# The last layer's residual: turned by DMA in 16-bit halves and added by DMA, instead of by TensorE transposes

## The chip, the cores and the metric

The kernel runs on one core of a Trainium2 chip. The metric is the device time of one execution in microseconds (us); the median of several executions is compared. One execution of each kernel was also recorded by the hardware profiler, and all rows shown here come from such a record. TensorE is PE in the rows (PEld its weight loads), VectorE is DVE, ScalarE is ACT, GpSimd is POOL, and SyncE, which only issues DMAs in this kernel, is SP.

## The reference

Two layers on a sequence of 1024 tokens with 1024 channels, everything in float32. Layer 0 is a gated delta-rule attention, layer 1 a chunked softmax attention; each is followed by the same convolutional FFN. What matters here is the end of layer 1:

```python
def conv_ffn(xn, w_up, conv_w, conv_b, w_down):
    h = causal_dwconv(xn @ w_up, conv_w) + conv_b
    gate, val = h[..., :FFN_DIM], h[..., FFN_DIM:]
    return (jax.nn.silu(gate) * val) @ w_down
...
        h = h + conv_ffn(rmsnorm(h, f_norm[layer]), f_w_up[layer], f_conv[layer], f_conv_b[layer], f_w_down[layer])
    return rmsnorm(h, final_norm)
```

The output has tokens in rows. The `h` that is added in the last line but one is the residual this text is about. Inside the kernel it lies with channels on the 128 partitions and tokens along the free axis, so that it has to be transposed before the final norm.

## The kernel before

Both FFNs are written by one function, `ffn(layer, ...)`. Every float32 product is made of three matmuls on a high and a low part (`uh`/`ul` from the raw up-weights `r`, `dh`/`dl` from the raw down-weights `a`, `eh`/`el` from the gated hidden rows `val`): high times high, low times high, high times low. ACT casts the high part, POOL or DVE subtracts to get the low part. The up-product and the down-product are done by a scheme of seven half-size products (n = 1 to 7) in place of eight.

The order of work is written by hand. `step(key, f)` appends one piece of PE work to the list `seq`; nearly every step is 12 matmuls with 512 columns. `at(i, f, rank)` hangs work for the other engines and DMA issues onto step i; at each step the jobs are emitted by rank, then the PE work. Each engine runs its own instructions in the order of emission and waits where an input is not there. SP's queue is such an order too: a DMA behind one that waits for a buffer is issued after it.

- `load` (L1492) and `load_a` (L1755) issue the weight loads on SP, some steps ahead.
- `product` and `second` are the up- and down-products on PE. The result of `second` is copied to `stage` and sent by POOL (`send`, L1817, and `send_e`, L1824) with an accumulating DMA into the DRAM tiles `d_c`, which gather the down-product of groups 0 to 8 (two hidden tiles of 128 channels each, 18 of the 22; the last four are done apart).
- `end` is the last step of the up-products. After it come the steps `("f", t)`: for each of the eight token tiles t the last four hidden tiles times their down-weights (`fw`, cut into `fh`/`fl` by `cut_last`), accumulated in PSUM tiles `pf`. These are laid out with tokens on the partitions already.
- Before the change, each pair (t, half c) of `pf` starts with the residual: `load_r` loads a 128x4x128 piece of `d_r` (the DRAM copy of the residual that layer 1's attention wrote, `d_r1`), and `tile_of` transposes it on PE into the PSUM tile with `is_transpose=True` (L1974), so that the products add onto it.
- `load_t` (L1944) loads the gathered sums of token tile t from `d_c` into the SBUF tile `fh[t]` (called `ht` in the rows). `closing(t)` adds the PSUM tile onto it on DVE and then runs the steps of the final norm `norm_out`: the squares on ACT, the reciprocal and the scaling on DVE, the output DMAs on SP.

At the start of the kernel the input x is turned in a similar way to what the change now does for the residual: DMA transposes of x seen as 16-bit halves into `xm` (L1280), a store to DRAM (L1282), a load of the halves (L1291), and copies of each half to every second 16-bit place (L1299). There POOL and DVE make the copies.

Of the kernel before, what the change touches and what calls it, by code (L numbers as in the profile page):

```python
# [9 lines left out]
F32 = mybir.dt.float32  # L10
# [6 lines left out]
P = 128  # L17
# [11 lines left out]
def trunk_kernel(  # L29
# [92 lines left out]
    def hs(s):  # L122
        return slice(s * HALF, (s + 1) * HALF)
# [375 lines left out]
    ctx_h = ExitStack()  # L499

    d_r0 = {(c, s, u): dram.tile([P, SEQ], F32, name=f"d_r0{c}{s}{u}") for c in range(2) for s in range(2) for u in range(2)}
    d_r1 = {(c, s): dram.tile([P, 2 * SEQ], F32, name=f"d_r1{c}{s}") for c in range(2) for s in range(2)}
    quarter = lambda d, m, s: d[m // 4, s, m % 4 // 2][:, hs(m % 2)] if (0, 0, 0) in d else d[m // 4, s][:, hs(m % 4)]
    d_y = [[dram.tile([P, HALF], F32, name=f"d_y{k}_{s}") for s in range(2)] for k in range(KT)]
    d_z = [[dram.tile([P, HALF], F32, name=f"d_z{k}_{s}") for s in range(2)] for k in range(KT)]
# [901 lines left out]
    def ffn(layer, h, hp, xs, tail, d_r, last):  # L1407
# [475 lines left out]
        if layer == 0:  # L1883

            def part(s, m, ks):
                def f():
                    if ks[0] == 0:
                        if s == 0 and m > 3:
                            if m % 2 == 0:
                                fps["d"] = pacc.tile([P, SEQ], F32, name="pf", tag="d", bufs=2)  # L1890
                            fps[s, m] = fps["d"][:, hs(m % 2)]
                        else:
                            fps[s, m] = pacc.tile([P, HALF], F32, name="pf", tag="u", bufs=4)
                    for k in ks:
                        triple(fps[s, m], fw[m], [t_[:, hs(s)] for t_ in hid[k0 + k]], kc[k], k == 0, k == 3)
                        if (s, m, k) in ((1,5,3),(1,6,2)):
                            next(norms[0])
                return f

            def closing(s, m):  # L1900
                def f():
                    tt(nc.vector, fh[m][:, hs(s)], fps[s, m], fh[m][:, hs(s)], add)
                    nc.sync.dma_start(out=d_h[m][:, hs(s)], in_=fh[m][:, hs(s)])
                    if m == 0:
                        norms.append(norm_steps(fh, s, None, last))
                    next(norms[s])
                    if s == 1 and m > 5:
                        for _ in range((2, 8)[m - 6]):
                            next(norms[0], None)
                return f  # L1910

            for m in range(KT):
                step(("f", 0, m, 0), part(0, m, range(3)))
            for m in range(KT):
                step(("f", 0, m), part(0, m, range(3, 4)))
            for m in range(KT):
                step(("f", 1, m), part(1, m, range(4)))
            for s in range(2):
                for m in range(KT):
                    at(pos["f", s, m | 1 if s == 0 and m > 3 else m] + 1, closing(s, m), 0)  # L1920

            def fin_h():
                for m in range(KT):
                    fh[m] = fin.tile([P, SEQ], F32, name=f"h{m}", tag=f"h{m}")
                for s in range(2):
                    for m in range(KT):
                        nc.sync.dma_start(out=fh[m][:, hs(s)], in_=quarter(d_c, m, s))
                rooms = [x for _ in range(3) for x in ("uh", "ul")]

                def tmp():  # L1930
                    rooms.append(rooms.pop(0))
                    return wf.tile([P, HALF], F32, name="nt", tag=rooms[-1], bufs=3)

                env["tmp"] = tmp
                env["acc"] = lambda s: wf.tile([P, HALF], F32, name="nacc", tag="dh", bufs=2)
                env["aux"] = lambda name: pacc.tile([P, SEQ], F32, name=name, tag="d", bufs=2)

            at(end, fin_h, 3)
        else:

            def load_t(t):
                fh[t] = fin.tile([P, SEQ], F32, name=f"ht{t}", tag=f"ht{t}")
                for c in range(2):
                    nc.sync.dma_start(out=fh[t][:, hs(c)], in_=d_c[c, t // 4, t % 4 // 2][:, hs(t % 2)])  # L1944

            res = {}

            def load_r(t):

                for c in range(2):  # L1950
                    if t < 4:
                        tag = ("eh", "el", "dh", "dl")[t % 2 * 2 + c]
                        r_ = (wd if tag[0] == "e" else wf).tile([P, 4, P], F32, name="res", tag=tag, bufs=2)
                    else:
                        r_ = actp.tile([P, 4, P], F32, name="res", tag=f"x{'hl'[c]}{t}_1")
                    nc.sync.dma_start(out=r_, in_=d_r[c, t // 4].rearrange("p (f t) -> p f t", f=4)[:, :, kc[t % 4]])
                    res[t, c] = r_

            def tile_of(t, ks):
                def f():  # L1960
                    if ks[0] == 0:
                        if t in (0, 1, 4, 5):
                            ps = pacc.tile([P, SEQ], F32, name="pf", tag="d", bufs=2)
                            fps[t] = [ps[:, hs(c)] for c in range(2)]
                        else:
                            fps[t] = [pacc.tile([P, HALF], F32, name="pf", tag="u", bufs=4) for _ in range(2)]
                            if t == KT - 1:
                                fps[t].append(pacc.tile([P, SEQ], F32, name="pf", tag="d", bufs=2))
                    for c in range(2):
                        parts = [(fps[t][c], 0, HALF)] if (t, c) != (KT - 1, 1) else [(fps[t][1 + q], 256 * q, 256) for q in range(2)]  # L1970
                        for ps, o, n in parts:
                            if ks[0] == 0:
                                for f in range(n // P):
                                    nc.tensor.matmul(ps[:, f * P : (f + 1) * P], res[t, c][:, o // P + f], ident, is_transpose=True, start=f == 0, stop=False, skip_group_check=True)  # L1974
                            for k in ks:
                                hh, hl = [x_[:, t * P : (t + 1) * P] for x_ in hid[k0 + k]]
                                hi, lo = [x_[:, o : o + n] for x_ in fw[2 * k + c]]
                                mm(ps[:, 0:n], hh, hi, start=False, stop=False, skip_group_check=True)
                                mm(ps[:, 0:n], hh, lo, start=False, stop=False, skip_group_check=True)
                                mm(ps[:, 0:n], hl, hi, start=False, stop=k == 3, skip_group_check=True)  # L1980
                return f

            its = {}

            def closing(t):
                def f():
                    its[t] = last(t, fh[t], fin)
                    if t == KT - 1:
                        tt(nc.vector, fh[t][:, hs(0)], fps[t][0], fh[t][:, hs(0)], add)
                        next(its[t - 1], None)  # L1990
                        next(its[t])
                        for q in range(2):
                            part = fh[t][:, HALF + 256 * q : HALF + 256 * (q + 1)]
                            tt(nc.vector, part, fps[t][1 + q][:, 0:256], part, add)
                            next(its[t], None)
                        return
                    for c in range(2):
                        tt(nc.vector, fh[t][:, hs(c)], fps[t][c], fh[t][:, hs(c)], add)
                    next(its[t])
                    if t > 0:  # L2000
                        next(its[t - 1], None)
                return f

            for t in range(4):
                step(("f", t, 0), tile_of(t, range(3)))
            for t in range(4):
                step(("f", t), tile_of(t, range(3, 4)))
            for t in range(4, KT):
                step(("f", t), tile_of(t, range(4)))
            at(end, lambda: last(None, None, fin), 3)  # L2010
            for t in range(KT):
                at(pc[t] if t < 4 else end + 1, lambda t=t: load_r(t), 3.5)
                at(end, lambda t=t: load_t(t), 4)
                at(pos["f", t] + 1, closing(t), 0)

        with tc.manual_schedule():
            for i in range(len(seq) + 8):
# [32 lines left out]
    with ExitStack() as ph:  # L2050
# [402 lines left out]
        def rest(s):  # L2453
# [20 lines left out]
            for m in range(KT):  # L2474
# [8 lines left out]
                nc.vector.tensor_tensor(h[m][:, hs(s)], ps, h[m][:, hs(s)], op=ALU.add)  # L2483

                def then(s=s, m=m):
                    nc.scalar.dma_start(out=quarter(d_r1, m, s), in_=h[m][:, hs(s)])
                    if m == 0:
                        its[s] = norm_steps(h, s, g_f[:, 1], normed, keep=True, gap=s == 0)
                    next(its[s])
# [153 lines left out]
```

## Time and profile before

| what | value |
|---|---|
| median of 3 executions | 2516.37 us (2515.14 to 2516.85) |
| the profiled execution: its time, its span in the trace | 2516.6 us, 2514.9 us |
| TensorE clock granted | 0.998 |
| busy share of the span: PE, DVE, POOL, ACT | 99%, 73%, 60%, 56% |
| packets on SP's DMA queue | 228.77 MB, 31.0% of the 16 DMA engines' span |
| packets of POOL's DMAs (nearly all accumulating) | 94.38 MB, 21.0% |

The span is the time from the first to the last instruction of the trace; the 1.7 us between it and the execution's own time lie before and after. In a timeline row stand the start in us, the duration, the engine, the line, the operation, out<-in, the shape, and in brackets how long the engine was idle before it and what ended that. In a row on DMAs "to landing" is the time from issue to the arrival of the data. Layer 1's FFN runs from about 1880 us to the end, and the steps ("f", t) from 2456.8 us.

### The profile page before, as it was taken

The page shows a single profiled execution, that of the slowest core. Times are in us where ns is not written, and L with a number is a line of the kernel's source. Part 1 is how long each engine was busy: PE and PEld are TensorE (multiplying, and loading weights), DVE is VectorE, ACT ScalarE, POOL GpSimd, SP SyncE. Part 2 cuts the span into 40 slices and gives each one's busy share as a digit, 9 for nine tenths or more (in the row PEclk, how much of TensorE's full clock was granted, in tenths as well). Part 3 has the DMA queues.
Part 4 walks back from the last instruction along what each step waited for, and adds up shares of the span by engine and source line. Part 5 has one row for each costly group of instructions (what it writes and reads, how often), then busy time and mean ns, then how long its engine had stood idle before and what let it go on. Part 6 is the DMA issues. An engine that isn't in the chain of part 4 may idle for free.

```text
span 2514.9 us, 39318 instructions
## 1 busy us (share of the span) xinstructions
PE 2483.2 (99%) x13905; PEld 2070.7 (82%) x13905; DVE 1835.3 (73%) x2984; ACT 1408.7 (56%) x2708; POOL 1496.6 (60%) x1523
## 2 busy tenths in 40 slices
PE   8999999999999999999999999999999999999999
PEld 6888888888878888888888888888877888888877
DVE  5765774456798888888866556667489788888884
ACT  6444555464465556565555556566456555655553
POOL 3655553357457777777635544445444777777770
PEclk9999999999999999999999999999999999999999
DMA  8743444554347777767832111122432667777795
GB/s 227 190 116 105 133 128 146 162 184 148 100 106 145 151 153 152 152 143 158 190 133 63 54 57 49 49 68 79 139 101 92 157 142 153 151 153 150 153 197 187
DMA packets 334101, 334.31 MB, mean 133 GB/s; under 512 B 50000, under 2 KB 256336, under 8 KB 333904
## 3 DMA queue, kind: packets, MB, share of 16 engines
q1 hardware_dynamic: 303232, 228.77, 31.0%
q0 software_dynamic: 25920, 94.38, 21.0%
q10 hardware_dynamic: 4752, 8.65, 1.0%
q8 instruction: 109, 1.79, 0.3%
q14 instruction: 88, 0.72, 0.1%
HBM read 180.68 MB, written 146.87 MB: 130 GB/s over the span
## 4 chain that ended last, share of the span: by engine, by line
PE 90%; POOL 3%; issue 2%; DVE 2%; ACT 1%; DMA 1%; SPq 0%; POOLq 0%; DVEq 0%; ACTq 0%
PE pu L1448 9%; PE pu L1446 9%; PE pu L1447 9%; PE acc L118 8%; PE acc L119 8%; PE acc L120 8%; PE pd L1447 4%; PE pd L1448 4%; PE pd L1446 4%; PE acco L118 2%; PE acco L120 2%; PE acco L119 2%; PE ptp L2272 2%; POOL ul L1412 1%; PE poT L2318 1%
## 5 line engine op out<-in xcount | busy, mean ns | idle before, releaser
L1412 POOL TENSOR_TENSOR ul<-r,uh 128x512 fp32r<-128x512 f32 x267 | 429.9, 1629 | 260.2 <-ACT uh L1434 255.3
L118 PE MATMUL acc<-xh,whi 128*128 128x512 f32 x896 | 374.9, 419 | 0.6 <-ACT xh L1094 0.6
L119 PE MATMUL acc<-xl,whi 128*128 128x512 f32 x896 | 352.3, 393 | 0.5 <-POOL xl L381 0.4
L120 PE MATMUL acc<-xh,wlo 128*128 128x512 f32 x896 | 351.9, 393 | 0.0
L103 POOL TENSOR_TENSOR wlo<-wraw,whi 128x256 fp32r<-128x256 f32 (+1 forms) x326 | 238.4, 761 | 140.1 <-ACT whi L101 132.8
L1434 ACT CAST uh<-r 128x512 fp32r<-128x512 f32 x289 | 177.3, 622 | 183.8 <-DVE r L1412 153.3
L1448 PE MATMUL pu<-xh,ul 128*128 128x512 f32 x524 | 204.6, 390 | 0.9 <-POOL ul L1412 0.9
L1446 PE MATMUL pu<-xh,uh 128*128 128x512 f32 x524 | 204.4, 390 | 0.7 <-ACT keep L1575 0.7
L1802 ACT COPY stage<-pd 128x1024 f32<-128x1024 f32 x180 | 175.3, 1013 | 53.0 <-PE pd L1448 51.6
L1447 PE MATMUL pu<-xl,uh 128*128 128x512 f32 x524 | 203.9, 389 | 0.0
L120 PEld LDWEIGHTS acc<-xh,wlo 128*128 128x128 f32 x896 | 168.5, 188 | 37.7
L119 PEld LDWEIGHTS acc<-xl,whi 128*128 128x128 f32 x896 | 169.6, 189 | 25.3 <-POOL xl L381 2.4
L118 PEld LDWEIGHTS acc<-xh,whi 128*128 128x128 f32 x896 | 169.3, 189 | 24.2 <-ACT xh L1094 1.0
L2227 POOL TENSOR_SCALAR sS<-sS,st 128x640 f32<-128x640 f32 (+4 forms) x128 | 86.0, 677 | 173.2 <-DVE st L2225 161.3
L1412 POOL TENSOR_TENSOR dl<-a,dh 128x512 fp32r<-128x512 f32 x90 | 151.9, 1687 | 53.6 <-ACT dh L1434 42.3
L1541 DVE SCALAR_TENSOR_TENSOR gate<-gpre,colt,gate 128x1023 f32<-128x1023 f32 (+2 forms) x92 | 173.3, 1884 | 3.2 <-ACT gate L1538 2.4
L1541 DVE SCALAR_TENSOR_TENSOR val<-vpre,colt,val 128x1023 f32<-128x1023 f32 x88 | 147.7, 1678 | 28.9 <-ACT val L1538 28.8
L2217 DVE CUSTOM_DVE_ANT_0 sS<-sc,bt 128x640 f32<-128x640 f32 (+4 forms) x128 | 84.2, 658 | 111.3 <-PE sc L2213 86.6
L1412 DVE TENSOR_TENSOR r<-r,r 128x512 f32<-128x512 f32 x160 | 130.3, 814 | 31.2 <-POOL ul L1412 30.1
L1412 DVE TENSOR_TENSOR el<-val,eh 128x512 fp32r<-128x512 f32 x90 | 86.0, 955 | 43.3 <-ACT eh L1434 43.3
L1448 PEld LDWEIGHTS pu<-xh,ul 128*128 128x128 f32 x524 | 98.3, 188 | 23.3 <-POOL ul L1412 1.8
L1446 PEld LDWEIGHTS pu<-xh,uh 128*128 128x128 f32 x524 | 98.4, 188 | 21.2 <-ACT keep L1575 1.1
(422 smaller groups left out, 7161.7 us busy)
## 6 DMA issues: line engine op xcount, KB each, us to landing
r<-in_f_w_up_dram SPq DMA_DIRECT2D x176, 256.0 KB, 4.3
d_r<-stage POOLq DMA_DIRECT2D x78, 512.0 KB, 7.9
d_c<-stage POOLq DMA_DIRECT2D x70, 512.0 KB, 8.0
a<-in_f_w_down_dram SPq DMA_DIRECT2D x72, 256.0 KB, 2.7
wraw<-in_a_w_in_dram SPq DMA_DIRECT2D x32, 512.0 KB, 4.6
d_e<-stage POOLq DMA_DIRECT2D x32, 512.0 KB, 9.2
wraw<-in_a_w_out_dram SPq DMA_DIRECT2D x16, 512.0 KB, 3.9
d_r<-h ACTq DMA_DIRECT2D x32, 256.0 KB, 2.5
```

Of the source, the lines that this page charges most:

```text
L103: nc.gpsimd.tensor_tensor(lo[:, c], raw[:, c], hi[:, c].bitcast(F32), op=ALU.subtract)
L118: mm(ps, hi[:, kw, wcol : wcol + P], rh[k][s], start=st, stop=False)
L119: mm(ps, hi[:, kw, wcol : wcol + P], rl[k][s], start=False, stop=False)
L120: mm(ps, lo[:, kw, wcol : wcol + P], rh[k][s], start=False, stop=sp)
L1412: tt = lambda eng, o, a, b, op: eng.tensor_tensor(o, a, b, op=op)
L1434: copy(hi, src)
L1446: mm(ps, w[0][:, cw], x[0], start=first, stop=False, skip_group_check=True)
L1447: mm(ps, w[0][:, cw], x[1], start=False, stop=False, skip_group_check=True)
L1448: mm(ps, w[1][:, cw], x[0], start=False, stop=last, skip_group_check=True)
L1541: nc.vector.scalar_tensor_tensor(t_[:, a:c1], p_[:, a - step : c1 - step], w[:, 2 - step : 3 - step], t_[:, a:c1], op0=ALU.mult, op1=ALU.add)
L1802: nc.scalar.copy(t_, ps)
L2227: nc.gpsimd.tensor_scalar(S, S, st[:, 3:4], 1.0, op0=ALU.mult, op1=ALU.mult)
```

## The change

The residual is stored row by row in one DRAM tile, turned during layer 1's FFN, and loaded into the final tiles as float32 with tokens on the partitions. The gathered sums `d_c` are then added onto it in SBUF by accumulating DMAs of POOL. The transposes on PE and their loads are gone, and the first matmul of each `pf` tile starts the accumulation.

```diff
-    d_r1 = {(c, s): dram.tile([P, 2 * SEQ], F32, name=f"d_r1{c}{s}") for c in range(2) for s in range(2)}
+    d_r1 = dram.tile([SEQ, SEQ], F32, name="d_r1")
...
             def load_t(t):
                 fh[t] = fin.tile([P, SEQ], F32, name=f"ht{t}", tag=f"ht{t}")
+                nc.sync.dma_start(out=fh[t], in_=d_rj[t])
+
+            def add_t(t):
                 for c in range(2):
-                    nc.sync.dma_start(out=fh[t][:, hs(c)], in_=d_c[c, t // 4, t % 4 // 2][:, hs(t % 2)])
-
-            res = {}
-
-            def load_r(t):
-
-                for c in range(2):
-                    if t < 4:
-                        tag = ("eh", "el", "dh", "dl")[t % 2 * 2 + c]
-                        r_ = (wd if tag[0] == "e" else wf).tile([P, 4, P], F32, name="res", tag=tag, bufs=2)
-                    else:
-                        r_ = actp.tile([P, 4, P], F32, name="res", tag=f"x{'hl'[c]}{t}_1")
-                    nc.sync.dma_start(out=r_, in_=d_r[c, t // 4].rearrange("p (f t) -> p f t", f=4)[:, :, kc[t % 4]])
-                    res[t, c] = r_
+                    nc.gpsimd.dma_start(out=fh[t][:, hs(c)], in_=d_c[c, t // 4, t % 4 // 2][:, hs(t % 2)], accum_op=add)
+
+            U16 = mybir.dt.uint16
+            d_rt = [dram.tile([2 * SEQ, HALF], U16, name=f"d_rt{c}") for c in range(2)]
+            d_rj = [dram.tile([P, SEQ], F32, name=f"d_rj{t}") for t in range(KT)]
+            rows_u = d_r.bitcast(U16)
+            turned, parts_r = {}, {}
+
+            def turn_r(b, c):
+                turned[b, c] = tp.tile([P, HALF], U16, name="rm", tag="rm", bufs=2)
+                nc.sync.dma_start(out=turned[b, c], in_=rows_u[hs(c), b * P : (b + 1) * P], transpose=True)
+
+            def put_r(b, c):
+                nc.sync.dma_start(out=d_rt[c][b * P : (b + 1) * P], in_=turned[b, c])
+
+            def load_r(t, c, q):
+                r_ = parts_r[t, c, q] = tp.tile([P, 2, 256], U16, name="rm", tag="rm", bufs=2)
+                nc.sync.dma_start(out=r_, in_=d_rt[c].rearrange("(t h) c -> t h c", h=2)[t * P : (t + 1) * P, :, q * 256 : (q + 1) * 256])
+
+            def join_r(t, c, q):
+                r_ = parts_r[t, c, q]
+                f_ = parts_r[t, c, q] = tp.tile([P, 256], F32, name="rj", tag="rm", bufs=2)
+                hm = f_.bitcast(U16).rearrange("p (t h) -> p t h", h=2)
+                for i in range(2):
+                    nc.scalar.copy(hm[:, :, i], r_[:, i])
+
+            def send_r(t, c, q):
+                nc.sync.dma_start(out=d_rj[t][:, c * HALF + q * 256 : c * HALF + (q + 1) * 256], in_=parts_r[t, c, q])
...
-                            if ks[0] == 0:
-                                for f in range(n // P):
-                                    nc.tensor.matmul(ps[:, f * P : (f + 1) * P], res[t, c][:, o // P + f], ident, is_transpose=True, start=f == 0, stop=False, skip_group_check=True)
...
-                                mm(ps[:, 0:n], hh, hi, start=False, stop=False, skip_group_check=True)
+                                mm(ps[:, 0:n], hh, hi, start=k == 0, stop=False, skip_group_check=True)
...
-                at(pc[t] if t < 4 else end + 1, lambda t=t: load_r(t), 3.5)
                 at(end, lambda t=t: load_t(t), 4)
+                at(end + 2, lambda t=t: add_t(t), 4.5)
                 at(pos["f", t] + 1, closing(t), 0)
+            i = pos["p", 3, 7]
+            for o in range(16):
+                for c in range(2):
+                    at(i, lambda o=o, c=c: turn_r(o, c), 3.2)
+                    at(i + 2, lambda o=o, c=c: put_r(o, c), 3.2)
+                    i += 2
+            i += 2
+            for t in range(KT):
+                for c in range(2):
+                    for q in range(2):
+                        at(i, lambda t=t, c=c, q=q: load_r(t, c, q), 3.2)
+                        at(i + 2, lambda t=t, c=c, q=q: join_r(t, c, q), 2.6)
+                        at(i + 3, lambda t=t, c=c, q=q: send_r(t, c, q), 3.1)
+                        i += 3
```

The first place that moves is ScalarE in the middle of the layer, where the 32 joins stand between the casts, seven of them in a period of 57 us that repeats. These are its instructions at one place of that period, before:

```order
L1538 ACTIVATE gate<-gpre,colt 128x1024
L1575 COPY keep<-pu_22380 128x512
L1434 CAST uh<-r_22166 128x512
L1434 CAST dh<-a_21932 128x512
L1434 CAST eh<-val 128x512
L1434 CAST uh<-r_22214 128x512
L1434 CAST uh<-r_22351 128x512
```

And the same place after (`rm` are the loaded halves, `rj` the joined float32 piece):

```order
L1971 COPY rj<-rm 128x256 x2
L1575 COPY keep<-pu_22542 128x512
L1434 CAST uh<-r_22310 128x512
L1434 CAST dh<-a_22055 128x512
L1434 CAST eh<-val 128x512
L1434 CAST uh<-r_22361 128x512
L1971 COPY rj<-rm 128x256 x2
L1434 CAST uh<-r_22510 128x512
```

Two copies stand ahead of the drain `keep` and its cast, and two more ahead of the cast of the next weights, six instructions later.

The second place is SP's queue at the same time, before:

```order
L1492 DMA r_22351<-in_f_w_up_dram 128x4x128
L1755 DMA a_22353<-in_f_w_down_dram 128x512
L1755 DMA a_22355<-in_f_w_down_dram 128x512
L1492 DMA r_22425<-in_f_w_up_dram 128x4x128
L1755 DMA a_22427<-in_f_w_down_dram 128x512
L1492 DMA r_22449<-in_f_w_up_dram 128x4x128
```

And after, where the first `r` is the same load as the first one above:

```order
L1492 DMA r_22510<-in_f_w_up_dram 128x4x128
L1755 DMA a_22512<-in_f_w_down_dram 128x512
L1755 DMA a_22514<-in_f_w_down_dram 128x512
L1974 DMA d_rj_19543<-rj 128x256
L1964 DMA rm<-d_rt_19540 128x2x256
L1492 DMA r_22590<-in_f_w_up_dram 128x4x128
L1755 DMA a_22592<-in_f_w_down_dram 128x512
L1492 DMA r_22617<-in_f_w_up_dram 128x4x128
L1974 DMA d_rj_19543<-rj 128x256
L1964 DMA rm<-d_rt_19540 128x2x256
```

The store of a joined piece, which waits for ScalarE, and the next load of halves now stand between the weight loads.

The third place is POOL behind its last subtractions, before:

```order
L1412 TENSOR_TENSOR ul<-r_24540,uh 128x512
L1412 TENSOR_TENSOR fl_24719<-fr,fh_24718 128x512
L1412 TENSOR_TENSOR fl_24794<-fr,fh_24793 128x512
L2558 TENSOR_TENSOR ht_24777<-ht_24777,g_fin 128x512
L2639 UNCONDITIONAL_BRANCH
```

And after:

```order
L1412 TENSOR_TENSOR fl_24998<-fr,fh_24997 128x512
L1412 TENSOR_TENSOR fl_25065<-fr,fh_25064 128x512
L1947 DMA ht_25035<-d_c_19477 128x512
L1947 DMA ht_25035<-d_c_19481 128x512
L1947 DMA ht_25037<-d_c_19477 128x512
L1947 DMA ht_25037<-d_c_19481 128x512
```

Sixteen accumulating DMAs follow the last subtraction on POOL, of which the first four are shown; before, POOL had nothing to do there until the end.

More of the change, by code (lines that the diff above doesn't have):

```diff
@@ L2485, in then @@
                 def then(s=s, m=m):
-                    nc.scalar.dma_start(out=quarter(d_r1, m, s), in_=h[m][:, hs(s)])
+                    nc.scalar.dma_start(out=d_r1[m * P : (m + 1) * P, hs(s)], in_=h[m][:, hs(s)])
                     if m == 0:
```

## The prediction

> **What bounds the kernel now.** I read the page first, then the busy time by stretch, then PE's and DVE's timelines at the end.
>
> ```profile
> span 2514.9 us, 39318 instructions
> PE 2483.2 (99%) x13905; PEld 2070.7 (82%) x13905; DVE 1835.3 (73%) x2984; ACT 1408.7 (56%) x2708; POOL 1496.6 (60%) x1523
> PE 90%; POOL 3%; issue 2%; DVE 2%; ACT 1%; DMA 1%; SPq 0%; POOLq 0%; DVEq 0%; ACTq 0%
> ```
>
> PE is busy for 99% of the span and makes 90% of the chain that ended last. The kernel gets shorter only by work taken off PE, or longer by waits that PE does not have now. The stretches of layer 1's FFN (columns: PE, PEld, DVE, ACT, POOL busy, granted clock, DMA share, GB/s) say where there is room:
>
> ```profile
> 2060.00:2120.00 60.00, 59.88 (x264) 49.20 (x264) 51.15 (x48) 35.70 (x51) 47.04 (x35) 1.00 0.69 145
> 2360.00:2400.00 40.00, 39.95 (x176) 32.57 (x175) 33.63 (x29) 21.38 (x29) 32.16 (x26) 1.00 0.91 185
> 2440.00:2456.00 16.00, 15.23 (x67) 12.64 (x68) 12.38 (x9) 7.43 (x12) 9.55 (x6) 1.00 1.10 297
> 2456.00:2480.00 24.00, 24.00 (x123) 19.73 (x122) 8.52 (x13) 4.78 (x9) 1.73 (x2) 1.00 0.82 259
> ```
>
> In the middle PE loses 0.1 us in 60, at 264 matmuls, so a step of 12 is 2.73 us. ACT is busy for 60% of it, and the DMA engines for 69%. With the DMA share at 0.91 PE still loses only 0.05 us in 40. From 2456 us on PE never stops.
>
> **The transposes leave PE.** The timeline of PE at the end:
>
> ```profile
> 2456.77 0.60 PE L1974 MATMUL pf<-ident,res 128*128 128x128 f32 x4
> 2459.29 0.60 PE L1974 MATMUL pf<-ident,res 128*128 128x128 f32 x4
> 2476.93 0.39 PE L1978 MATMUL pf<-fh,hidh 128*128 128x512 f32 x1
> 2482.54 0.60 PE L1974 MATMUL pf<-ident,res 128*128 128x128 f32 x4
> 2485.76 0.60 PE L1974 MATMUL pf<-ident,res 128*128 128x128 f32 x4
> ```
>
> Four transposes and 9 matmuls take 2459.29 - 2456.77 = 2.52 us. Between 2476.93 and 2482.54 stand the 24 matmuls of the last k of tiles 0 to 3, which have no transposes: 0.2338 us each. Nine of them make 2.10, so four transposes cost 0.42 us. Later, with 12 matmuls, it is 3.22 - 2.81 = 0.41. There are 16 such groups, 6.7 us in all. Not all of it reaches the end, as DVE shows:
>
> ```profile
> 2478.53 2.69 DVE L1412 TENSOR_TENSOR ht<-pf,ht 128x512 f32<-128x512 f32 x4 [11.47 <-PE pf L1980]
> 2495.64 1.29 DVE L1412 TENSOR_TENSOR ht<-pf,ht 128x512 f32<-128x512 f32 x2 [3.22 <-PE pf L1980]
> 2505.31 0.69 DVE L1412 TENSOR_TENSOR ht<-pf,ht 128x512 f32<-128x512 f32 x1 [1.01 <-PE pf L1980]
> 2507.44 0.42 DVE L1412 TENSOR_TENSOR ht<-pf,ht 128x256 f32<-128x256 f32 x1
> ```
>
> The closings wait for PE up to the first half of tile 7 at 2505.31; the next at 2507.44 comes with no idle time, behind DVE's scaling of tile 6. So 15 of the 16 groups count: 15 x 0.42 = 6.3 us. Bounds: 5.9 (14 groups) and 6.7.
>
> **The loads of `res` go.** Half of these 16 loads (4.2 MB) were issued before 2456 us, where the DMA engines have no room (share 1.10). PE's one large wait there:
>
> ```profile
> PE pul L1448 <- POOL ul L1412: 1.2, 1, 1.2
> POOL d_c L1824 <- DMA d_c<-stage: 5.5, 1, 5.5
> ```
>
> POOL stood 5.5 us for the landing of an accumulating DMA, and its next `ul` came 1.2 us late. Two `res` loads (0.5 MB) run beside that DMA and go. The gain lies between 0 and 1.2; I take 0.3, since 0.5 MB is a small part of what is in flight.
>
> **Turning and storing, 32 of each, on SP's queue.** A pair stands every second step, 5.4 us. Nearest rows are the transposes of x, of twice the size, each with its time to landing, and the first loads of halves:
>
> ```profile
> L1280 SPq DMA_TRANSPOSE xm<-in_x_dram x16: 1159/1292/6231, 11.6 to 73.2; - x16
> ...
> DMA to landing us min/median/max: 3.1/3.7/7.8
> L1291 SPq DMA_DIRECT2D xm<-d_xt x16: 529/540/1017, 80.8 to 636.8; - x16
> ...
> DMA to landing us min/median/max: 3.0/4.1/5.0
> ```
>
> A store waits for its transpose, so a pair holds SP for 3.7 us and the store's issue of about 0.4, which fits into 5.4. Behind it wait weight loads, and behind those ACT's casts. A typical one with little room:
>
> ```profile
> 2172.68 0.37 SPq L1492 DMA_DIRECT2D r<-in_f_w_up_dram  x1
> 2184.98 1.39 ACT L1434 CAST uh<-r 128x512 fp32r<-128x512 f32 x2
> ```
>
> The waits of SP's queue in the 12.7 us up to it (total, times, longest):
>
> ```profile
> SPq L1492 <- POOL ul L1412: 6.5, 1, 6.5
> SPq L1492 <- DVE r L1412: 1.2, 1, 1.2
> ```
>
> The load issued at 2172.68 feeds the second of these casts, at 2185.7: 13 us, of which some 4 are flight. Nine us are left for delay in the queue, two whole pairs. Three pairs stand ahead of such a load at the worst, of which the first store finds its data landed: 9 us by these rows, against the 6.5 + 1.2 = 7.7 that SP waits there for buffers now. I take 0; bounds 0 and 4 us (two such places, 2 us each).
>
> The traffic of the whole chain is four passes of 4.2 MB, 16.8 MB, over some 160 steps or 437 us. At the rate of SP's queue (228.77 MB in 31.0% of the span, 293 GB/s of engine time; rows below) that is 57 us, a share of 0.13: from 0.69 to about 0.82, under the 0.91 at which PE did not wait.
>
> **Joining, 32 times two copies on ACT.** ACT has a copy of this width in the norm's squares; DVE's joins of x are the same operation over 512 elements:
>
> ```profile
> 2507.94 0.42 ACT L2556 ACTIVATE jk<-ht 128x256 f32<-128x256 f32 x1 [0.85 <-DVE ht L1412]
> L1299 DVE COPY xs<-xm x16: 454/750/1285, 545.4 to 645.9; 128x512 uint16<-128x512 uint16 x16
> ```
>
> Two copies make 0.84 us, within DVE's 0.45 to 1.29 for as many elements; I take 0.84, ACT's own row. That is 27 us of ACT over 262 us, in which it is idle for 40%. It matters where the cast behind it has little time to reach PE, as at the `keep` in the place shown above:
>
> ```profile
> 2181.86 0.56 ACT L1575 COPY keep<-pu 128x512 f32<-128x512 f32 x1
> 2183.13 0.62 ACT L1434 CAST uh<-r 128x512 fp32r<-128x512 f32 x1 [0.70 <-DVE r L1412]
> 2183.83 1.75 POOL L1412 TENSOR_TENSOR ul<-r,uh 128x512 fp32r<-128x512 f32 x1 [1.46 <-ACT uh L1434]
> 2186.18 0.39 PE L1448 MATMUL pu<-xt2h,ul 128*128 128x512 f32 x1
> ```
>
> A delay of `keep` is first taken up by the 0.70 us for which ACT waits for DVE, then by the 0.60 between the end of `ul` (2185.58) and its use. That is 1.30 against 0.84: hidden, with 0.46 to spare. This is the tightest of the seven places that repeat. What can break it is the load of halves: issued when the store before it is, about 3 us before the second join of this place by the row of 2184.98, it lands after 4.1. ACT would stand 1 to 2 us there; but POOL is busy with the `ul` and `dl` before, and the cast has time. I put 0.5 us for all joins; bounds 0 and 7 (five `keep` places, 1.4 each).
>
> The page "DMA: Bandwidth & Descriptors" of the Trainium skill, section "Anatomy of one DMA", fits a DMA's time as 2.0 us and its bytes at 436 GB/s. As an estimate from that page, a load of 128 KB would land after 2.3 us and no join would wait, and the sum would end 0.5 us lower. The measured 4.1 (for 256 KB, where that fit gives 2.6) says that loads here take longer, and decides.
>
> **The gathered sums are added by POOL's DMAs.** The rows for it:
>
> ```profile
> q1 hardware_dynamic: 303232, 228.77, 31.0%
> q0 software_dynamic: 25920, 94.38, 21.0%
> q1 hardware_dynamic: 3072, 4.42, 105.3%
> L1817 POOL DMA_DIRECT2D d_c<-stage x64: 848/900/1493, 1981.4 to 2426.7; - x64
> 2452.12 11.57 SPq L1944 DMA_DIRECT2D ht<-d_c  x16
> 2461.14 1.29 POOL L1412 TENSOR_TENSOR fl<-fr,fh 128x512 fp32r<-128x512 f32 x1 [4.70 <-ACT fh L1874]
> ```
>
> The third row is the 12 us from 2452, nearly all `ht` loads: 4.42 MB, 368 GB/s. The accumulating DMAs run at 94.38 MB in 528 us, 179 GB/s. After the change SP starts the residual's 4.2 MB at 2452.1; with 0.9 MB of other loads they are in by 2466. POOL is free at 2462.4 and issues 16 DMAs at 0.9 us, until 2477. The adds need 4.2 MB / 179 = 23.5 us of the DMA engines; with about 1.8 done before 2466 and 2 us to land, tile t is complete at about 2469 + 3t: tile 0 at 2469, tile 3 at 2478, tile 7 at 2490. Needed are tile 0 at 2478.5 - 8 x 0.42 = 2475.2, tiles 1 to 3 at 1.4 us each behind it (2479.4), tile 7 at 2501.1. So the adds are hidden, with 11 us to spare at the end and hardly any at tile 3; a tile that is late there costs nothing, since DVE is idle between later closings. Bounds: nothing, if adding into SBUF runs as the sends into DRAM did; with half that rate tile 7 lands at 2513.2, 12.1 us too late. I take 0, the rate of the only accumulating rows.
>
> **The sum.** -6.3 (transposes) - 0.3 (`res`) + 0 (turning) + 0.5 (joins) + 0 (adds) = -6.1 us, from 2514.9 to 2508.8 of span. The profiled execution took 2516.6, 1.7 more than its span and 0.2 more than the median, so the median becomes 2516.37 - 6.1 = 2510.3.
>
> **Rivals.** First, the middle pays it back: ACT stands at the joins, or weight loads come late behind SP's stores. For it speaks that ACT runs in order and everything behind a join waits; against it the idle 40% of ACT. At its bound of 7 us, or half of that with the 4 us of turning, the time is 2512 to 2517: no measurable change.
>
> Second, slower: the adds end last. The place is closing of tile 7, the price 23.5 us times a factor for SBUF as the target. It costs nothing up to a factor of 1.48 (tile 7 at 2501.1), eats the whole gain at 1.75, and at 2 gives 2516.37 - 6.1 + 12.1 = 2522.4. For it: such a DMA is not in this trace, and its rows are 2 KB where the sends had 4 KB. Against it: the sends' rate already holds reads of the target, from DRAM.
>
> Third, a little more: all of POOL's 1.2 us wait goes and all 16 groups count, 2516.37 - 6.7 - 1.2 = 2508.5.
>
> **How the numbers follow.** The forecast's own range is 2508.9 to 2511.3, chance 0.60; the third case (2508 to 2508.9) 0.06; the first rival (2511.3 to 2517) 0.23; the adds last (2513 to 2525) 0.11. What can be told from no change is 0.2%, 5.0 us: faster is under 2511.3, slower over 2521.4. Faster 0.66; same 0.23 and about 0.02 of the adds, 0.25; slower 0.09. The range 2508.4 to 2517 leaves out most of the adds' case and the end of the third: it holds 0.87.
>
> **What would show it.** No L1974 of PE, the pitch of the `pf` groups at 2.10 and 2.81 us, and a last closing 6 us earlier: the first term. PE at 59.9 of 60 in the stretches from 1940 to 2360, with no row of PE waiting for ACT, POOL or DVE over 2 us in sum: the middle is hidden. No idle time of DVE's `ht` from tile 4 on that ends by a DMA: the adds are in time; such a row of several us at tile 7 means the second rival. The prediction is wrong if PE's busy share falls in the middle, or if the closings wait for `ht`.

## The result, and the profile after

The changed kernel is slower: 2525.58 us median of 22 executions (2516.32 to 2533.77), against 2516.76 of 22 before (2513.74 to 2521.48). The ratio is 1.0032, with a 95% interval of 1.0021 to 1.0042. The forecast was 2510.3, at most 2517. The profiled execution of the changed kernel took 2519.74 us, 5.8 less than the median, so its trace shows the kinds of loss, and less of it than most executions have.

The page of the changed kernel, the same three rows as shown of before:

```profile
span 2518.0 us, 39436 instructions
PE 2479.6 (98%) x13841; PEld 2063.7 (82%) x13841; DVE 1833.4 (73%) x2984; ACT 1429.1 (57%) x2772; POOL 1506.6 (60%) x1539
PE 80%; DMA 7%; issue 4%; POOL 4%; DVE 4%; ACT 2%; SPq 0%; ACTq 0%; DVEq 0%; POOLq 0%
```

PE's share of the chain that ended last fell from 90% to 80%, and DMA rose from 1% to 7%. The stretches say where (same columns as in the prediction; the last row is the kernel before, at the time of the second):

```profile
2060.00:2120.00 60.00, 57.52 (x248) 45.57 (x247) 45.01 (x45) 34.74 (x52) 42.29 (x33) 1.00 0.86 182
2180.00:2240.00 60.00, 57.08 (x248) 45.80 (x247) 46.39 (x45) 38.36 (x62) 43.21 (x33) 1.00 0.76 168
2360.00:2400.00 40.00, 40.00 (x177) 32.87 (x177) 33.89 (x32) 24.25 (x37) 30.38 (x26) 1.00 0.94 202
2456.00:2480.00 24.00, 23.84 (x105) 19.44 (x104) 16.47 (x18) 10.84 (x16) 12.64 (x13) 1.00 0.82 260
...
2180.00:2240.00 60.00, 59.99 (x264) 49.28 (x264) 49.80 (x48) 36.14 (x51) 46.23 (x34) 1.00 0.72 148
```

Before, PE did at least 264 matmuls in each 60 us of the middle; now it does 248 in two of them. Both kernels run the same 13,841 matmuls once the transposes are left out, so each can be matched with its own in the other trace. Its start after less its start before, worked out so:

```
matmul    before     after    after - before
 12065   2095.17   2096.36      +1.2
 12091   2101.35   2104.36      +3.0    while it is turned
 12139   2112.38   2116.38      +4.0    behind the first join
 12319   2153.18   2157.92      +4.7
 12595   2216.27   2225.69      +9.4
 13099   2331.33   2342.39     +11.1    joining, to 2372 us
 13567   2440.76   2450.44      +9.7    one PE wait of 1.2 us is gone
 13638   2457.44   2467.11      +9.7    the last products begin
 13701   2475.09   2481.39      +6.3
 13830   2507.11   2509.86      +2.8    the last tile
```

From the first of the last products on PE gains 6.9 us, where 6.3 was forecast; the span is 3.1 us longer than before, so 6.6 of the gain reach its end. The middle loses 11: it stands at +0.3 when turning begins at 1910 us, so some 3 us are lost while the residual is turned and 8 from the first join on. The waits of ScalarE and of PE that have to do with it, from 2060 to 2360 us (total, times, longest):

```profile
ACT rj L1971 <- DMA rm<-d_rt: 20.9, 11, 5.2
ACT rj L1971 <- DMA r<-in_f_w_up_dram: 3.2, 1, 3.2
PEld pu L1448 <- POOL ul L1412: 12.1, 13, 1.3
PE pu L1448 <- POOL ul L1412: 6.8, 11, 0.8
```

The second row is the first join, at 2113.67 us; the copies there read the halves whose load was issued at 2110.25, whatever the row names. The kernel before has the last two rows too, at 2.4 and 0.2 us. The largest of ScalarE's waits, on the timelines of ACT, POOL and PE:

```profile
2200.93 0.60 ACT L1434 CAST uh<-r 128x512 fp32r<-128x512 f32 x1
2206.68 0.82 ACT L1971 COPY rj<-rm 128x256 uint16<-128x256 uint16 x2 [5.15 <-DMA rm<-d_rt]
2207.83 0.63 ACT L1434 CAST uh<-r 128x512 fp32r<-128x512 f32 x1
...
2208.54 1.28 POOL L1412 TENSOR_TENSOR ul<-r,uh 128x512 fp32r<-128x512 f32 x1 [5.54 <-ACT uh L1434]
...
2208.51 0.50 PE L1446 MATMUL pu<-xh,uh 128*128 128x512 f32 x1 [0.77 <-ACT uh L1434]
2209.88 0.50 PE L1448 MATMUL pu<-xh,ul 128*128 128x512 f32 x1 [0.63 <-POOL ul L1412]
```

ScalarE is free at 2201.5 and stands 5.15 us at a join whose halves have not landed. The drain and the cast of the next weights stand behind it, POOL waits 5.54 us for the cast, and PE for both. ScalarE waits for halves at three of the seven places that repeat, the same three each time round: 1.2 to 2.8 us at the first, 1.7 to 5.2 at the second, and up to 1.3 at the third.

### The profile page after: what moved, and what is told of

The parts are those of the page before. It is cut to its first block, busy times and chain, and to the rows that moved or that the text cites. A ratio compares the mean times of both kernels' runs of the same rounds, so it can differ in the third digit from the quotient of the medians.

```text
span 2518.0 us, 39436 instructions
## 1 busy us (share of the span) xinstructions
PE 2479.6 (98%) x13841; PEld 2063.7 (82%) x13841; DVE 1833.4 (73%) x2984; ACT 1429.1 (57%) x2772; POOL 1506.6 (60%) x1539
## 4 chain that ended last, share of the span: by engine, by line
PE 80%; DMA 7%; issue 4%; POOL 4%; DVE 4%; ACT 2%; SPq 0%; ACTq 0%; DVEq 0%; POOLq 0%
PE acc L118 8%; PE acc L119 8%; PE acc L120 8%; PE pu L1448 7%; PE pu L1446 7%; PE pu L1447 7%; DMA rm<-d_r 4%; PE pd L1448 3%; PE pd L1447 3%; PE pd L1446 3%; PE acco L118 2%; PE acco L120 2%; PE acco L119 2%; PE ptp L2300 2%; POOL ul L1412 2%
```

## The experiments

Every run is an edit of the changed kernel. Line numbers of the rows can differ by a few from kernel to kernel.

**1. The end alone.**

```diff
-                nc.sync.dma_start(out=fh[t], in_=d_rj[t])
+                nc.sync.dma_start(out=fh[t], in_=d_r[t * P : (t + 1) * P])
...
-            i = pos["p", 3, 7]
-            for o in range(16):
-                for c in range(2):
-                    at(i, lambda o=o, c=c: turn_r(o, c), 3.2)
...
-                        at(i + 3, lambda t=t, c=c, q=q: send_r(t, c, q), 3.1)
-                        i += 3
```

> The whole chain of the middle (turning, storing, loading halves, joining, storing) is left out, and the final tiles are loaded from the untransposed rows of the residual, with the same packets; the transposes stay off PE and the accumulating DMAs stay. So the output holds a residual that is not turned. Theory A (the loss is all in the middle, the end gains what the trace of the changed kernel shows: 6.9 us there and 1.4 us near 2440 us): 2508.5 us, range 2507 to 2510.5, closings without a wait for DMA. Rival B (part of the loss comes from the end, for instance the accumulating DMAs): 2512 us or more.

2509.35 us (2506.86 to 2513.28), ratio 0.9972 (0.9963 to 0.9982). The end is worth 7.5 us, so by the medians the chain of the middle costs 2525.58 - 2509.35 = 16.2. PE's wait near 2440 us is still there with 1.3 us, though the `res` loads are gone here too. So the 1.4 us that the changed kernel's trace gains at that place can't be put down to those loads.

**2. Turning alone, and joining alone.** Both load the final tiles as run 1 does.

```diff
 turn only:  the loop over load_r, join_r, send_r left out
 join only:  the loop over turn_r, put_r left out, and
-                nc.sync.dma_start(out=r_, in_=d_rt[c]...)
+                nc.sync.dma_start(out=r_, in_=rows_u[t * P : (t + 1) * P, ...])
             (the copies then read every second place of the piece)
```

> As the run without the chain, but the 32 transposing DMAs and the 32 stores of their results stay; no loads of halves, joins or stores behind them. In the trace of the changed kernel PE lost 3.6 us in this part (up to 2116 us) and 7.0 in the joining part. Theory A (both parts cost, each by itself): 3 to 7 us over the run without the chain, 2511 to 2516 us, with PE's losses between 2060 and 2120 us. Rival B (only the joins cost, the loss in this part was chance): within 1 us of the run without the chain.

> As the run without the chain, but the 32 loads of halves, the joins of ScalarE and the 32 stores of the joined pieces stay, at the steps where they stand in the changed kernel; no transposing DMAs and no stores of theirs. The halves are pieces of rows, so the output is not the reference's. Theory A (the joins cost through ScalarE, which stands at a copy until late halves land): 7 to 11 us over the run without the chain, 2515.5 to 2520 us, and ScalarE waiting some 20 us for halves. Rival B (the late halves of the changed kernel come from stores and loads that depend on the turning): within 3 us of the run without the chain.

Turning alone: 2512.92 us (2508.38 to 2529.37), 3.6 over run 1. Joining alone: 2516.78 (2512.69 to 2522.85), 7.4 over it. Theory A holds in both, and in the second ScalarE stood 19.3 us for halves. The two make 11.0 of the 16.2 us. The 5.2 between them can't be told from noise: the 95% intervals of the four medians reach 2.3 to 3.4 us to each side, and by these the 3.6 alone is not clear of zero either. The profiled execution of turning alone is the longest of its kind and shows what can happen there (windows, then ACT's waits between 1900 and 2120 us):

```profile
2076.00:2084.00 8.00, 8.00 (x37) 6.62 (x36) 7.96 (x5) 3.07 (x4) 7.33 (x7) 1.00 1.07 180
2084.00:2092.00 8.00, 8.00 (x37) 6.62 (x36) 6.35 (x9) 5.80 (x8) 5.62 (x5) 1.00 1.31 91
2100.00:2108.00 8.00, 0.00 (x0) 0.00 (x0) 0.00 (x0) 0.08 (x1) 0.00 (x0) 0.57 1.12 192
2108.00:2116.00 8.00, 7.28 (x19) 5.30 (x20) 5.60 (x7) 5.32 (x8) 4.21 (x3) 0.58 0.53 136
...
ACT uh L1434 <- DMA r<-in_f_w_up_dram: 19.0, 2, 16.1
```

Four sends, a store, a transposing DMA and three weight loads are in flight soon after 2084 us, the DMA share is over 1, for 8 us only 91 GB/s move, one weight load keeps ScalarE waiting for 16.1 us, and PE does nothing for 11.3 us on end. Behind that wait it does 19 matmuls in 8 us, at a granted clock of 0.58, where it did 37 before.

**3. Copies or waits?** The first kernel loads pieces of the unturned rows and stores them without copying; the second makes the same copies from a tile that is always there.

```diff
 no copies:
-                for i in range(2):
-                    nc.scalar.copy(hm[:, :, i], r_[:, i])
+                parts_r[t, c, q] = r_.bitcast(F32).rearrange("p h c -> p (h c)")
 no wait:
-                    nc.scalar.copy(hm[:, :, i], r_[:, i])
+                    nc.scalar.copy(hm[:, :, i], rz)
```

> The whole chain with all its DMAs, but ScalarE copies nothing: the loaded piece is stored as it is, and SP waits for its landing where it waited for ScalarE. The pieces come from untransposed rows, so the output is not the reference's. Theory A (the joining part loses because ScalarE stands at a join): only the loss of the turning part stays, 2511 to 2516 us, and no wait of ScalarE for halves. Rival B (the DMAs delay weight loads, in SP's queue or in flight, whatever ScalarE does): as slow as the changed kernel, 2519 to 2526 us.

> The changed kernel, but the joins copy from a tile that lies in SBUF all the time instead of the loaded halves, so ScalarE makes the same 64 copies and never stands for a load; all DMAs stay. The residual in the output is zero. Theory A (standing for late halves is what the joins cost): as fast as the run without copies, 2514 to 2518 us. Rival B (the copies' own 0.84 us on ScalarE are the cost): no change, 2522 us or more.

2516.26 us (2508.87 to 2526.32) without copies, 2516.79 (2509.75 to 2525.9) with copies and no wait for halves: 9.3 and 8.8 less than the changed kernel. The first is 0.3 above theory A's range and well below rival B's. So the 27 us of copies cost nothing that can be told from noise (0.5 us between the two), and some 9 of the 16.2 us go with ScalarE's standing for loads. The traces say the same more sharply. PE's loss against the kernel before, worked out as in the table of matmuls, from 1900 to 2112 us and from 2112 to 2360 us by the times of before:

```
                     turning   joining
changed kernel         2.9       7.9
1  the end alone       0.1       0.1
2  turning alone      18.6       0.1
2  joining alone       0.1       6.1
3  no copies           2.0       0.3
3  no wait             5.8      -0.3
```

Without the standing the joining part loses nothing, though all its DMAs are there. Turning loses 2.0 to 18.6 us in the traces that have it, so its loss is real, and it differs widely from execution to execution. In the second kernel ScalarE still stands at the joins, for buffers (2110 to 2372 us):

```profile
ACT rj L1970 <- DMA d_rj<-rj: 14.2, 13, 2.5
```

14.2 us in pieces of up to 2.5 lose PE nothing there; in the changed kernel 26.4 us in pieces of up to 5.2 (23.2 in the row for halves, 3.2 in that of the first join) lost it 7.9 over the same stretch. I read this as the tolerance of each place counting, and not the sum; no run tests the places one by one.

**4. SP's queue.** The stores of the joined pieces are issued by ScalarE.

```diff
-                nc.sync.dma_start(out=d_rj[t][:, ...], in_=parts_r[t, c, q])
+                nc.scalar.dma_start(out=d_rj[t][:, ...], in_=parts_r[t, c, q])
```

> The changed kernel, but the 32 stores of the joined pieces are issued by ScalarE, right where its program has done the join, instead of by SP, which stood for ScalarE there for 140 us in 30 waits. Theory C (SP standing for joins delays the weight loads behind): 3 to 8 us faster than the changed kernel, 2517 to 2522 us. Theory A (ScalarE's standing for halves is the cost, SP's is not): within 3 us of the changed kernel, 2522.5 to 2528 us.

2524.96 us (2513.45 to 2546.3): no change. This run is a weak test, though: SP, freed of the store, stood no shorter at the load behind it (159 us in all). The rows of SP's standing at the store (2110 to 2372 us), in the changed kernel, in the kernel without the wait of run 3 and in that of run 5, say more:

```profile
SPq L1974 <- ACT rj L1971: 140.0, 29, 11.5
...
SPq L1973 <- ACT rj L1970: 126.4, 28, 7.0
...
SPq L1975 <- ACT rj L1972: 130.4, 26, 8.1
```

SP stands nearly as long where the joining part loses PE nothing, so theory C falls: SP's standing there costs little.

**5. Why the halves are late.** POOL's accumulating sends carry half of their columns; half of the sums are left out.

```diff
-                    nc.gpsimd.dma_start(out=total(n, u), in_=stage[g, n, u], accum_op=add)
+                    nc.gpsimd.dma_start(out=total(n, u)[:, w_], in_=stage[g, n, u][:, w_], accum_op=add)   # w_: 512 of 1024
```

> The changed kernel, but POOL's accumulating sends of the gathered sums in this layer carry half of their columns (256 KB each instead of 512), with as many instructions on every engine; half of the sums are left out, so the output is not the reference's. Theory A (halves and weights land late because they queue behind the sends' traffic): loads of halves land in about 3 us, ScalarE's standing for them falls from 23 us to under 6, and the time is 2509 to 2513 us. Rival B (they land late because of the order in SP's queue or of stores they depend on): 2520 us or more.

2508.74 us (2506.86 to 2510.66), ratio 0.9967 (0.9954 to 0.9979): the whole loss is gone, with the chain in place. In its trace PE loses 0.2 us in the turning part and -0.1 in the joining part. The spread is small as well, but these are five executions against 22. The loads of halves, time to landing from 2112 to 2372 us, in the changed kernel and in this one, and ScalarE's waits for them here:

```profile
DMA to landing us min/median/max: 2.5/5.2/12.3
...
DMA to landing us min/median/max: 2.4/3.4/6.0
...
ACT rj L1972 <- DMA rm<-d_rt: 0.9, 4, 0.2
```

The order in SP's queue, the stores that the loads depend on and POOL's time to issue a send (0.90 us against 0.95) are nearly the same, so theory A stands: the halves are late since they share the DMA engines with the sends, or the memory behind these; this run can't tell which. The Trainium skill, page "DMA: Bandwidth & Descriptors", section "Issuing engines are not separate DMA queues", says so as a rule: DMAs of scalar, sync and gpsimd run on the same 16 engines and interleave. Both this run and run 4 agree with it: another queue for the stores gave 0.6 us, half the sends' bytes 16.8. There is no run of half the sends without the chain; 1.4 us of what this trace gains lie at PE's wait near 2440 us, where the chain has no part.

**6. Turning where the sends are not.**

```diff
-            i = pos["p", 3, 7]
+            i = 2
... (the joins stay at their steps)
-                    at(i + 2, lambda o=o, c=c: put_r(o, c), 3.2)
-                    i += 2
+                    at(i + 1, lambda o=o, c=c: put_r(o, c), 3.2)
+                    i += 1
```

> The changed kernel with the 32 transposing DMAs and their stores begun at step 2 instead of step 23, one pair a step instead of every second, in a stretch with a DMA share of about 0.3; the joins stay where they are. Theory A (turning costs by being in the bursts of POOL's sends): its 3.6 us (and what it adds to the joins) go, 2518 to 2522 us. Rival B (turning costs wherever it stands, since SP waits for every transposing DMA): no change or slower, 2524 us or more.

2519.34 us (2515.79 to 2524.22), 6.2 less than the changed kernel: theory A. Turning costs less ahead of the first send. The joins keep their loss, 7.4 us in this trace. The landing of the transposing DMAs, in the changed kernel and in run 7, which has the same early turning:

```profile
DMA to landing us min/median/max: 2.4/4.2/11.5
...
DMA to landing us min/median/max: 2.4/2.6/5.0
```

**7. Joining where the sends are not.** With early turning, joins stand at four places of each period of 21 steps.

```diff
+            quiet = [46 + 21 * a + b for a in range(8) for b in (0, 3, 6, 9)]
+            for n_, i in enumerate(quiet):
+                t, c, q = n_ // 4, n_ // 2 % 2, n_ % 2
+                at(quiet[n_ - 1] + 1 if n_ else i - 4, lambda t=t, c=c, q=q: load_r(t, c, q), 3.2)
+                at(i, lambda t=t, c=c, q=q: join_r(t, c, q), 2.6)
+                at(i + 1, lambda t=t, c=c, q=q: send_r(t, c, q), 3.1)
```

> Early turning as in the run before, and the joins only at four of the seven places that repeat (the others are those at which the trace of the changed kernel shows ScalarE standing for halves), each load of halves issued right behind the store before it, up to 12 steps ahead of its join. Theory A (late halves and bursts are the whole loss): 2509 to 2512.5 us, within 3 us of the run without the chain. Rival B (copies on ScalarE and stores on SP's queue cost by themselves): 2515 us or more.

2512.17 us (2507.76 to 2518.08), ratio 0.9979 (0.9970 to 0.9989): faster than the kernel before by 4 to 5 us, with the whole computation, and 13.4 us faster than the change as it was made. Its loads of halves landed as follows (1980 to 2380 us), and ScalarE waited for none of these:

```profile
DMA to landing us min/median/max: 2.4/3.3/6.6
```

PE loses 0.1 us in its trace from 2112 to 2360 us. What is left over run 1 is 2.8 us; a part of it lies at 2409 to 2441 us, at the last joins, where PE falls 3.2 us behind in this trace. One join there, at 2409.56, stands 2.5 us for its halves.

**8. Three attempts at that rest.** The last joins are brought away from there by putting three, or one, ahead of the others.

```diff
 a:  quiet = [37, 40, 43] + [the places of 7][:29], the first load two steps ahead
 b:  as a, and each turn_r ahead of the put_r of the one before it
 c:  as b, with quiet = [43] + [the places of 7][:31]
```

> The version with early turning and quiet joins, with three joins more ahead of the first of POOL's sends, so that the last join stands 9 steps sooner and the last store is away from the loads at 2409 to 2440 us, where the trace of that version still lost 3 us. Theory A (that loss is the chain's last pieces): 2509 to 2511 us. Rival B (that loss is there by chance, as the 1.7 us at 1858 us are): as before it, 2511 to 2513 us.

> The version with three joins ahead of the sends lost 9 us where ScalarE stood 11.7 us at its first join, since the 32 pairs of turning held SP for 3.3 us each, to 1966 us, and the first load of halves was issued only then. Here each transposing DMA is issued ahead of the store of the one before it, so that SP stands less (by the rows of that trace some 2.3 us a pair, done at about 1935 us). Theory A: the first join finds its halves, and the time is 2508.5 to 2511 us. Rival B (joins that early cost, or turning that dense delays weight loads): 2513 us or more.

> The same order of turning, but only one join ahead of the others, at step 43. The last joins then stand at steps 196 and 199 instead of 199 and 202. Theory A: safe at the start, and part of the 3 us at 2409 to 2440 us stays: 2510 to 2512.5 us. Rival B (the loss there has nothing to do with the last joins): as the version with quiet joins, 2512 us, or more.

All three missed: a 2518.56 us (2515.24 to 2524.34), b 2521.41 (2517.79 to 2527.31), c 2516.73 (2512.22 to 2519.44). The timeline of ACT and SP in a, and of ACT in b:

```profile
1966.13 0.98 SPq L1492 DMA_DIRECT2D r<-in_f_w_up_dram  x1
1967.16 1.31 SPq L1964 DMA_DIRECT2D rm<-d_rt  x1
...
1972.34 0.81 ACT L1971 COPY rj<-rm 128x256 uint16<-128x256 uint16 x2 [11.72 <-DMA r<-in_f_w_up_dram]
...
1972.50 0.81 ACT L1971 COPY rj<-rm 128x256 uint16<-128x256 uint16 x2 [13.95 <-DMA r<-in_f_w_up_dram]
```

The wait is put down to `r`, but the load of halves issued at 1967.16 is what the copies read. It comes that late because 32 pairs of turning hold SP for 3.3 us each; b's order did not shorten that to 2.3, as I had worked out, since each transposing DMA then waits for the store that frees its buffer. In a and b one such wait costs 9 us, and the loss at 2409 us is gone, as theory A of a had it. PE itself waits only 5.5 us in a, but its granted clock is 0.50 from 1974 to 1977 us and 0.82 from there to 1985, and this costs the rest. Trace b loses 4 us more at 1945, where ScalarE stands for `stage` buffers whose stores have not landed. In c part of the loss at 2409 us stays, and 3.7 us come to it between 1967 and 1990, behind a down-weight load for which ScalarE stood 7.5 us. The rest has a place, but no version here removes it at less than it costs.

## Why the prediction was wrong

- **Transposes, -6.3 us: right, and a little small.** PE gained 9.67 - 2.76 = 6.9 us from the first of the last products to the last, 0.48 and 0.44 for the groups of 9 and 12 matmuls against the 0.42 worked out; 6.6 reach the end of the span. The group of 9 now takes 9 x 0.2267 = 2.04 us; I had taken the pitch of 0.2338 from a stretch that runs slightly slower. Run 1 is 7.5 us faster, against -6.6 for the terms of the end.
- **`res`, -0.3: unsettled and small.** The wait went in the changed kernel and stayed in run 1.
- **Adds, 0: right**, and with it the second rival wrong. The rows of the adding DMAs and the closings of tiles 0, 1 and 7:

```profile
L1947 POOL DMA_DIRECT2D ht<-d_c x16: 872/1610/3719, 2472.6 to 2487.6; - x16
DMA to landing us min/median/max: 4.0/10.0/12.0
...
2484.82 2.69 DVE L1412 TENSOR_TENSOR ht<-pf,ht 128x512 f32<-128x512 f32 x4 [7.54 <-PE pf L1994]
2508.52 0.69 DVE L1412 TENSOR_TENSOR ht<-pf,ht 128x512 f32<-128x512 f32 x1 [0.57 <-PE pf L1994]
```

  The first DMA lands at 2476.6 (2472.6 + 4.0), the last at 2499.6, so 15 of 0.26 MB take 23.0 us, 171 GB/s: the rate of the sends into DRAM, less a little. Closings wait for PE and never for a DMA, and tile 7 has 9 us to spare.
- **Joining, +0.5: the step that failed.** It was the flight of a load of halves, "it lands after 4.1", taken from loads of x between 80 and 637 us, where POOL sends nothing. The `r` loads of the very stretch, in the trace of before (2112 to 2372 us), were the row to use:

```profile
DMA to landing us min/median/max: 2.9/4.4/12.7
```

  The median, 4.4, says nearly the same; the longest says 12.7, and halves then had 2.5, 5.2 and 12.3. The load of 2194.23 us was given 7.3 us, until ScalarE was free for its join at 2201.5; it flew 12.3, and the difference is the 5.15 us of standing. The wait of 1 to 2 us that I named at the second join of the `keep` place, and let pass, came as named (1.3 us in that round, 1.2 to 2.8 in all). The one of 5.2 was at the next join, at which I had not looked. By the traces the joins cost PE 7.9 us, above the bound of 7. What I priced with care, the copies against 1.30 us of tolerance, was right: their cost can't be told from nothing. The estimate of 2.3 us that I set beside the sum, from the Trainium skill, page "DMA: Bandwidth & Descriptors", section "Anatomy of one DMA", is near the shortest flight of the stretch, 2.5; the page gives its fit for DMAs that GpSimd issues, and these loads are SP's.
- **Turning, 0: too low**, 3.6 us alone by the medians, 2.0 to 18.6 by the traces, against a bound of 4. The row of the transposes of x has a median of 3.7 and a longest of 7.8; here it was 4.2 and 11.5. The delay I looked for was SP's; what shows in the traces is the flight of the weight loads beside it, for one of which ScalarE stands 3.4 us in the changed kernel and 16.1 in run 2.
- **The share of 0.82 "under the 0.91 at which PE did not wait": the reason behind both.** The volume was right (0.86 and 0.76 in the rows above), but a mean over 60 us hides bursts. The kernel before, in windows of 8 us:

```profile
2052.00:2060.00 8.00, 8.00 (x37) 6.64 (x36) 5.68 (x6) 4.55 (x7) 6.66 (x5) 1.00 0.13 35
2076.00:2084.00 8.00, 8.00 (x37) 6.64 (x36) 7.96 (x7) 3.97 (x6) 5.61 (x6) 1.00 1.08 221
2084.00:2092.00 8.00, 8.00 (x38) 6.60 (x36) 4.79 (x6) 4.54 (x6) 6.19 (x5) 1.00 1.02 207
```

  For 16 us there was no room at all, and 16 us earlier stand 8 us that were nearly empty. Runs 6 and 7, which move the work to other steps, and run 5, which thins the bursts, agree with this. And 0.91 at 2360 to 2400 us was no limit: the changed kernel had 0.94 there and lost nothing.
- **The first rival was the case**, with a chance of 0.23 and an end of 2517. Its price was too small in the same way: even both bounds in full, 7 and 4 us, would have given 2521. By the medians the middle cost 16.2.

Left open: whether both parts together cost more than each by itself, and why executions differ by 17 us; the loss of turning, 2.0 to 18.6 us in the traces, varies by as much. The five executions of run 5 differ by 3.8, which suggests that the spread needs the sends in full.

## What to carry to other kernels

A transfer on whose landing an in-order engine will stand is priced by the longest flight among its neighbours in the same stretch, not by a median from a quiet part of the kernel, and room on the DMA engines is read in windows as short as one burst. When such work is added to a kernel whose traffic comes in bursts, first ask at which steps of the period the bursts are; moving the same 128 DMAs and 64 copies to the quiet steps turned 1.0032 into 0.9979. Moving work earlier only helps if what it needs is there: a join ahead of its data cost 9 us at a single place.

## What was not expected of the hardware

A load of 128 KB took 2.4 us to land in the quiet and 12.3 beside four accumulating sends of 512 KB; with sends of 256 KB its longest was 6.0. The Trainium skill, page "DMA: Bandwidth & Descriptors", section "Queues, rings and completion order", states that each DMA engine goes round its queues packet by packet. I had read that as a load passing the sends ahead of it, but taking turns sets no bound on the flight, which was longer than the sends' own median of 7.8 in that stretch; no run here takes the 12.3 us apart. Transposing DMAs of 128 KB hold SP's queue for 1.12 us each at least. In run 2 the engines moved 91 GB/s for 8 us at a share of 1.31, which no run here explains.

A long wait of PE cost more than its length. In run 2 PE waited 11.3 us and fell 14.7 behind, in run 8a it waited 5.5 and fell 8.9 behind, with the granted clock near 0.5 just after; the waits of the changed kernel, of up to 0.8 us, cost at most 0.2 more than they lasted.
